# Moving an indexer's choice of keys ahead of the latent up-projections, and filling latent heads to 128 rows

## The chip, the cores and the metric

The kernel runs on one core of a Trainium2 chip. The metric is the device time of one execution in microseconds (us). An engine's instructions run in the order of its queue; the order is laid out when the kernel is built. The engines are TensorE (PE; its weight loads are listed as PEld), VectorE (DVE), ScalarE (ACT), GpSimd (POOL) and SyncE (SP, which issues the loads of weights).

## The reference, cut to what matters

Two blocks of two layers each run one after the other on 256 positions of width 1024, all in float32. The first block has feed-forward parts, window attention and retention, and the change does not touch it. A layer of the second block projects its input, runs three kinds of attention side by side, gates the result, projects it out and normalizes. The change concerns two of the three:

- Latent attention has 6 heads. The queries come from a normalized vector of 768 values through an up-projection, the keys and values from one of 256. A head's query and key are 64 plain values and 32 rotated ones, 96 in all.
- Sparse attention has 4 heads. An indexer picks for each query the 64 best keys, and only those take part:

```python
logits = einsum('bqhd,bsd->bqhs', qib, k_idx) * IDX_DIM ** -0.5
score = einsum('bqh,bqhs->bqs', wb * IDX_HEADS ** -0.5, relu(logits))
score = where(key_pos <= qpos, score, -inf)
_, idx = top_k(score, topk)
```

The third kind, dilated attention with 6 heads, follows behind both.

## The kernel before, in words

A stage is one part of one layer; stages follow each other, and the two last stages, one for each layer of the second block, are those of class `Mixer2`. Positions lie in two tiles of 128 (tile 0 and tile 1). Products with weights are exact to float32 through three products of high and low parts: `get_at` (lines 298 to 308) loads a piece of weights, ScalarE writes its high part (line 304) and VectorE its low part (line 306). Eight buffers of each part let two groups of weights be in work. Results of TensorE go to eight banks: two with the name `mm` for projections, two `tr` for transposes, four `ac` for scores and attention outputs. Each bank has to be emptied by ScalarE or VectorE before its next use.

Nobody writes the order of a queue out by hand. The program issues instructions in the order of its text, and the builder lays out each engine's queue by its own estimate of when each instruction can start. `issue_after` ties some instructions behind others where the author wanted that.

`Mixer2.body` (line 1165) runs, in the order of its text:

- the indexer's query projection (`post2`), transposes of the latent vectors, then `post3` (indexer and sparse keys) and `post4` (line 1192: rotated latent key, the indexer's head weights, sparse values);
- the latent query up-projection, lines 1202 to 1214: two halves by two tiles, each in one `mm` bank, emptied by one ScalarE copy and by the four VectorE steps of `rope` (lines 647 to 650);
- the latent key and value up-projection, lines 1215 to 1226, also four `mm` banks;
- the transposes of queries and keys, lines 1236 to 1240, 96 columns to a head, into the tiles qT and kT, of which 96 partitions are used;
- latent scores (`a_score`, from `make`, line 1088): a matmul for each head with 96 rows, then `softmax` (line 652), whose first VectorE step, line 655, empties the bank;
- between them `choose(0)` (line 1278) and `choose(1)` (line 1283), and behind each the next projections as they fit.

`choose` (line 1041) makes the selection of one tile. TensorE multiplies 8 indexer heads in pairs on 64 rows each (line 1053); ScalarE takes the relu into one of two buffers `rl` (line 1057); VectorE adds the heads up with their weights in a chain of eight steps (lines 1063 and 1065), adds the causal mask, and then finds 64 keys in eight rounds: the top 8 (line 1069) and their replacement by a low value (line 1070). Two more steps make a mask. The sparse scores `c_score(0)` and `c_score(1)` (lines 1293 and 1298) use these masks.

Of the kernel before, what the change touches and what calls it, by code (L numbers as in the profile page):

```python
# [9 lines left out]
F32 = mybir.dt.float32  # L10
# [929 lines left out]
class Mixer2(OutProj, Attn):  # L940
# [100 lines left out]
    def choose(self, t, qiT):  # L1041

        K, nc = self.K, self.K.nc
        nk = 128 + 128 * t
        nh = 512 // nk
        acc = self.scr.tile([128, 256], F32, tag=f"acc{t}", name="acc")[:, :nk]
        cau = K.cau[:, 0:128] if t == 0 else K.cau[:, 128:384]
        for p0 in range(0, 4, nh):
            ps = [K.bank("ac", 4) for _ in range(2)]
            for j in range(nh):  # L1050
                for e in range(2):
                    r = slice(64 * e, 64 * e + 64)
                    K.mm(ps[e][:, nk * j:nk * j + nk], lhsT=qiT[r, p0 + j, 128 * t:128 * t + 128], rhs=self.kiT[r, :nk],
                         start=True, stop=True)
            for e in range(2):
                rl = self.rl[:, e]
                nc.scalar.activation(out=rl, in_=ps[e], func=AF.Relu, scale=0.125)
                for j in range(nh):
                    h = 2 * (p0 + j) + e
                    r = rl[:, nk * j:nk * j + nk]  # L1060
                    w = self.wi[:, t, h:h + 1]
                    if h == 0:
                        nc.vector.tensor_scalar(out=acc, in0=r, scalar1=w, scalar2=None, op0=ALU.mult)
                    else:
                        nc.vector.scalar_tensor_tensor(out=acc, in0=r, scalar=w, in1=acc, op0=ALU.mult, op1=ALU.add)  # L1065
        nc.vector.tensor_tensor(out=acc, in0=acc, in1=cau, op=ALU.add)
        m8 = K.small([8], "m8", 4)
        for _ in range(8):
            nc.vector.max(out=m8, in_=acc)  # L1069
            nc.vector.match_replace(out=acc, in_to_replace=m8, in_values=acc, imm_value=-3.0e38)  # L1070
        nc.vector.tensor_scalar(out=acc, in0=acc, scalar1=-2.0e38, scalar2=NEG, op0=ALU.is_gt, op1=ALU.mult)
        nc.vector.tensor_tensor(out=acc, in0=acc, in1=cau, op=ALU.add)
        self.sel[t] = acc
# [91 lines left out]
    def body(self):  # L1165
        K, nc, d = self.K, self.K.nc, self.K.d
        scr = self.scr
# [30 lines left out]
            self.copy(0, self.vc[:, t, :], ps[:, 40:296])  # L1198

        self.proj(post4)  # L1200

        for j in range(2):
            p = K.get(2)
            for t in range(2):
                ps = K.bank("mm")
# [10 lines left out]
        for t in range(2):  # L1216
            for j in range(2):
                ps = K.bank("mm")
# [6 lines left out]
                else:  # L1225
                    self.copy(1, self.va[:, t, :], ps[:, :384])

        self.rl = self.keep.tile([128, 2, 512], F32, tag="ch0", name="rl")
        self.al = self.keep.tile([128, 2, 512], F32, tag="cl0", name="al")
        self.n_al = 0  # L1230
        qbT = self.keep.tile([128, 4, 256], F32, tag="ch1", name="qbT")
# [1 line left out]
        vb = vbt.rearrange("p a n -> p (a n)")[:, :768].rearrange("p (t n) -> p t n", t=2)  # L1233
        qT = self.keep.tile([128, 6, 256], F32, tag="qT", name="qaT")
        kT = scr.tile([128, 6, 256], F32, tag="kT", name="kaT")
        for t in range(2):
            for dst, src, e in ((qT, qa[t], 0), (kT, ka[t], 1)):
                for h0, n in ((0, 4), (4, 2)):
                    ps = K.transposes([src[:, 96 * h:96 * h + 96] for h in range(h0, h0 + n)])
                    self.copy(e, dst[:96, h0:h0 + n, ts(t)], ps[:96, :128 * n].rearrange("p (h n) -> p h n", h=n))  # L1240
        self.y = [scr.tile([128, 4, 256], F32, tag=f"cqx{a}", name=f"y{a}") for a in range(2)]
        a_score, a_av = self.make(6, (64 + 32) ** -0.5, lambda h, s, q=qT: q[:96, h, s],
                                  lambda h, nk, k=kT: k[:96, h, :nk], self.va, 0, self.caus, False)
        half = lambda x: lambda h, s: x[64 * (h % 2):64 * (h % 2) + 64, h // 2, s]
        keys = lambda x: lambda h, nk: x[64 * (h % 2):64 * (h % 2) + 64, h // 2, :nk]
        c_score, c_av = self.make(4, 0.125, half(self.qcT), keys(self.kcT), self.vc, 3,
# [28 lines left out]

        a_score(0)
        a_score(1)
        self.choose(0, self.qiT)
        self.proj_T(4, post5)
        self.together(a_av(0), a_av(1))  # L1280
        a_score(2)
        a_score(3)
        self.choose(1, self.qiT)
        a_score(4)
        kbT = scr.tile([128, 3, 256], F32, tag="kT", name="kbT")

# [22 lines left out]
        for q in range(2):  # L1309
            ps = K.bank("tr")  # L1310
            for i in range(4):
                k = 16 + 4 * q + i
# [80 lines left out]
```

## Time and profile before

| | us |
|---|---|
| median of 3 runs | 1330.25 |
| lowest and highest | 1329.29, 1332.18 |
| the profiled execution, own time | 1329.58 |
| its span, first to last instruction | 1327.8 |
| busy: TensorE, VectorE, ScalarE, GpSimd | 1308.1, 1022.9, 741.2, 25.2 |
| mean granted TensorE clock | 0.998 |

Times in the trace count from the span's start. Matmuls are pipelined: a matmul's duration is longer than the step to the next one's start, so steps between starts are what a group costs. A float32 product without the split shows as two records. The stage of the first layer lies at about 966 to 1138 us, that of the second one about 178 us later. A row of the timeline merges neighbours of one kind: its first number is the start, the second the time to the end of the last one.

### The profile page before, as it was taken

How to read it: one execution, taken by the hardware profiler on the slowest of the kernel's cores; microseconds unless marked ns; L12 is line 12 of the kernel's file. 1: busy time of each engine (PE TensorE's matmuls, PEld its weight loads, DVE VectorE, ACT ScalarE, POOL GpSimd, SP SyncE). 2: the span in 40 equal slices, each digit the busy share in tenths (PEclk: the TensorE clock that was granted, in tenths of full speed). 3: DMA queues.
4: the chain of work that ended last, by engine and by line, in shares of the span. 5: the costliest groups of instructions: out<-in, count | busy, mean ns of one | idle time of the engine just before them, and what ended most of it. 6: DMA issues, size and time to landing. Idle time of an engine off the chain costs nothing. (4 is left out here: it accounts for less than half of the span.)

```text
span 1327.8 us, 20378 instructions
## 1 busy us (share of the span) xinstructions
PE 1308.1 (99%) x7606; PEld 1128.1 (85%) x7606; DVE 1022.9 (77%) x1753; ACT 741.2 (56%) x1312; POOL 25.2 (2%) x34
## 2 busy tenths in 40 slices
PE   9999999999999999999999999999999999999997
PEld 8888887888888888888887878888889898799886
DVE  7777669978976769787589777677585797866976
ACT  7755536446544546555355555545455678356681
POOL 0000000000000000000000000000000000000000
PEclk9999999999999999999999999999999999999999
DMA  9987624637867728877433548678355434364420
GB/s 330 342 302 266 211 75 143 211 123 259 310 234 260 252 81 327 278 263 249 151 128 114 204 139 286 206 269 275 127 176 181 139 127 145 126 209 160 142 81 33
DMA packets 75923, 263.39 MB, mean 198 GB/s; under 512 B 9104, under 2 KB 10384, under 8 KB 75696
## 3 DMA queue, kind: packets, MB, share of 16 engines
q1 hardware_dynamic: 74736, 259.75, 57.2%
q0 software_dynamic: 512, 1.69, 0.4%
q8 instruction: 59, 0.97, 0.3%
q10 hardware_dynamic: 576, 0.66, 0.1%
q14 instruction: 40, 0.33, 0.1%
HBM read 261.01 MB, written 1.05 MB: 197 GB/s over the span
## 5 line engine op out<-in xcount | busy, mean ns | idle before, releaser
L306 DVE TENSOR_TENSOR wlo<-st,whi 128x1024 fp32r<-128x1024 f32 (+5 forms) x320 | 372.3, 1174 | 66.6 <-ACT whi L304 66.3
L304 ACT ACTIVATE whi<-st 128x1024 fp32r<-128x1024 f32 (+5 forms) x320 | 322.8, 1018 | 115.3 <-DMA st<-in_w 45.7
L327 PE MATMUL mm<-xx,whi 128*128 128x256 f32 (+1 forms) x1296 | 333.7, 333 | 0.0
L327 PE MATMUL mm<-xx,wlo 128*128 128x256 f32 x928 | 261.7, 283 | 0.0
L327 PEld LDWEIGHTS mm<-xx,whi 128*128 128x128 f32 x1296 | 220.2, 190 | 24.2 <-issue 0.3
L327 PE MATMUL mm<-whi,xx 128*128 128x512 f32 (+3 forms) x744 | 219.4, 372 | 0.6 <-DVE xx L374 0.4
L327 PE MATMUL tr<-xx,whi 128*128 128x512 f32 x560 | 195.8, 392 | 0.0
L327 PEld LDWEIGHTS mm<-xx,wlo 128*128 128x128 f32 x928 | 176.6, 190 | 2.0 <-DVE wlo L306 0.4
L327 PE MATMUL tr<-xx,wlo 128*128 128x256 f32 x560 | 156.6, 280 | 0.0
L327 PEld LDWEIGHTS mm<-whi,xx 128*128 128x128 f32 x744 | 135.0, 188 | 24.8 <-DVE xx L374 1.7
L306 DVE TENSOR_TENSOR xlo<-st,xhi 128x1024 fp32r<-128x1024 f32 x106 | 128.4, 1218 | 18.8 <-ACT xhi L304 18.1
L304 ACT ACTIVATE xhi<-st 128x1024 fp32r<-128x1024 f32 x106 | 109.9, 1054 | 50.5 <-PE ac L327 39.2
L327 PE MATMUL mm<-wlo,xx 128*128 128x512 f32 (+3 forms) x372 | 137.1, 369 | 0.0
L327 PE MATMUL ac<-xlo,hth 128*128 128x512 f32 x320 | 125.6, 393 | 0.0
L327 PE MATMUL ac<-xhi,hth 128*128 128x512 f32 x320 | 125.4, 392 | 0.0
L327 PEld LDWEIGHTS tr<-xx,whi 128*128 128x128 f32 x560 | 104.8, 187 | 23.1
L327 PEld LDWEIGHTS tr<-xx,wlo 128*128 128x128 f32 x560 | 105.9, 189 | 1.3
L327 PE MATMUL ac<-xhi,htl 128*128 128x512 f32 x320 | 104.4, 391 | 0.0
L316 DVE SCALAR_TENSOR_TENSOR st<-st,sc 128x1024 f32<-128x1024 f32 x48 | 58.6, 1222 | 53.2 <-DMA st<-in_w 53.1
L327 PEld LDWEIGHTS mm<-wlo,xx 128*128 128x128 f32 x372 | 70.1, 188 | 10.6 <-issue 0.3
L373 ACT ACTIVATE hth<-sa 128x256 fp32r<-128x256 f32 x76 | 31.4, 413 | 79.1 <-DVE sa L538 79.0
L327 PEld LDWEIGHTS ac<-xhi,hth 128*128 128x128 f32 x320 | 60.1, 188 | 14.3
(271 smaller groups left out, 1829.0 us busy)
## 6 DMA issues: line engine op xcount, KB each, us to landing
st<-in_w SPq DMA_DIRECT2D x441, 512.0 KB, 4.6
st<-in_w SPq DMA_DIRECT2D x20, 384.0 KB, 3.6
g<-in_lng SPq DMA_DIRECT2D x8, 512.0 KB, 4.5
b<-in_lnb SPq DMA_DIRECT2D x8, 512.0 KB, 5.6
st<-in_w SPq DMA_DIRECT2D x8, 432.0 KB, 4.0
st<-in_w SPq DMA_DIRECT2D x8, 296.0 KB, 4.7
st<-in_w SPq DMA_DIRECT2D x5, 256.0 KB, 5.5
x<-in_x SPq DMA_DIRECT2D x2, 512.0 KB, 7.7
```

The source lines that it names most:

```text
L304: nc.scalar.activation(out=hi[:, :m], in_=st[:, :m], func=AF.Copy)
L306: nc.vector.tensor_tensor(out=lo[:, :m], in0=st[:, :m], in1=hi[:, :m].bitcast(F32), op=ALU.subtract)
L316: nc.vector.scalar_tensor_tensor(out=st, in0=st, scalar=1.0, in1=self.sc, op0=ALU.mult, op1=ALU.mult, accum_out=self.mod[l][:, j:j + 1])
L327: return self.nc.tensor.matmul(*a, **k).ins
L373: nc.scalar.activation(out=hi, in_=src, func=AF.Copy)
```

## The change

`choose` for both tiles moves from among the latent scores to just behind `post4`, ahead of the latent up-projections. Tile 0 takes its two banks from `tr`, tile 1 its four from `ac`. The relu buffers become three, and they lie in the memory that kT takes afterwards. Apart from that, qT and kT have their last 32 partitions cleared on GpSimd; the transposes take 128 columns (the last head 96), and the latent scores 128 rows.

```diff
         nk = 128 + 128 * t
         nh = 512 // nk
+        tag = (("tr", 2), ("ac", 4))[t]
         acc = self.scr.tile([128, 256], F32, tag=f"acc{t}", name="acc")[:, :nk]
...
-            ps = [K.bank("ac", 4) for _ in range(2)]
+            ps = [K.bank(*tag) for _ in range(2)]
...
-                rl = self.rl[:, e]
+                rl = self.rl[:, self.n_rl % 3]
+                self.n_rl += 1
...
         self.proj(post4)
+        self.rl = scr.tile([128, 3, 512], F32, tag="kT", name="rl")
+        self.n_rl = 0
+        self.choose(0, self.qiT)
+        self.choose(1, self.qiT)
...
-        self.rl = self.keep.tile([128, 2, 512], F32, tag="ch0", name="rl")
...
         kT = scr.tile([128, 6, 256], F32, tag="kT", name="kaT")
+        for a in (qT, kT):
+            nc.gpsimd.memset(a[96:128], 0.0)
...
-                    ps = K.transposes([src[:, 96 * h:96 * h + 96] for h in range(h0, h0 + n)])
+                    ps = K.transposes([src[:, 96 * h:min(96 * h + 128, 576)] for h in range(h0, h0 + n)])
...
-        a_score, a_av = self.make(6, (64 + 32) ** -0.5, lambda h, s, q=qT: q[:96, h, s],
-                                  lambda h, nk, k=kT: k[:96, h, :nk], self.va, 0, self.caus, False)
+        a_score, a_av = self.make(6, (64 + 32) ** -0.5, lambda h, s, q=qT: q[:, h, s],
+                                  lambda h, nk, k=kT: k[:, h, :nk], self.va, 0, self.caus, False)
...
         a_score(0)
         a_score(1)
-        self.choose(0, self.qiT)
         self.proj_T(4, post5)
         self.together(a_av(0), a_av(1))
         a_score(2)
         a_score(3)
-        self.choose(1, self.qiT)
         a_score(4)
```

## Rows read from the trace of the kernel before

**Rows 1.** The page, busy time of each engine over the span (share, instructions).

```profile
PE 1308.1 (99%) x7606; PEld 1128.1 (85%) x7606; DVE 1022.9 (77%) x1753; ACT 741.2 (56%) x1312; POOL 25.2 (2%) x34
```

**Rows 2.** Busy time by stretch: PE, PEld, DVE, ACT, POOL (instructions), granted clock, DMA share, GB/s.

```profile
1020.00:1030.00 10.00, 10.00 (x77) 10.00 (x77) 8.96 (x24) 6.13 (x10) 0.00 (x0) 1.00 0.67 218
1030.00:1040.00 10.00, 9.95 (x71) 9.28 (x70) 6.45 (x14) 5.98 (x11) 0.00 (x0) 1.00 0.55 172
...
1060.00:1070.00 10.00, 10.00 (x80) 9.85 (x80) 9.86 (x34) 9.04 (x21) 0.00 (x0) 1.00 0.01 2
```

**Rows 3.** TensorE's waits, 966 to 1138: us in total, times, longest.

```profile
PE ac L327 <- ACT PT L687: 0.9, 2, 0.5
```

**Rows 4.** Timeline of TensorE around tile 0's indexer scores.

```profile
1040.04 1.06 PE L327 MATMUL ac<-kaT,qaT 96*128 96x128 f32 x8
1041.03 1.16 PE L327 MATMUL ac<-kk,qiT 64*128 64x128 f32 x16
1042.12 0.38 PE L327 MATMUL mm<-xx,wlo 128*128 128x256 f32 x1
```

**Rows 5.** Timeline of TensorE around tile 1's indexer scores (idle time before, and its releaser).

```profile
1056.90 1.56 PE L327 MATMUL ac<-kk,qiT 64*128 64x256 f32 x10
1058.98 1.13 PE L327 MATMUL ac<-kk,qiT 64*128 64x256 f32 x6 [0.53 <-DVE P L655]
1060.04 1.13 PE L327 MATMUL ac<-kaT,qaT 96*128 96x256 f32 x4
```

**Rows 6.** Weight loads by line, 1030 to 1055: busy us, mean ns, idle before.

```profile
L442 PEld LDWEIGHTS tr<-idn,ka 128*96 128x96 f32 x12 | 1.2, 126 | 0.4 <-ACT qaT L1037 0.4
...
L442 PEld LDWEIGHTS tr<-idn,P 128*128 128x128 f32 x6 | 0.7, 140 | 0.0
```

**Rows 7.** Timeline of VectorE with both choices under way.

```profile
1060.21 0.08 DVE L1070 MATCH_VALUE_LOAD acc<-m,acc 128x8 f32 x1
1060.29 0.27 DVE L1070 MATCH_REPLACE8 acc<-m,acc 128x128 f32<-128x128 f32 x1
1060.48 0.47 DVE L1065 SCALAR_TENSOR_TENSOR acc<-rl,kk,acc 128x256 f32<-128x256 f32 x1
1060.87 0.28 DVE L1069 MAX8 m<-acc 128x8 f32<-128x128 f32 x1
1061.08 0.48 DVE L1065 SCALAR_TENSOR_TENSOR acc<-rl,kk,acc 128x256 f32<-128x256 f32 x1
```

**Rows 8.** Timeline of VectorE, tile 0's choice beside latent scores.

```profile
1058.06 0.28 DVE L1069 MAX8 m<-acc 128x8 f32<-128x128 f32 x1
1058.26 0.67 DVE L655 SCALAR_TENSOR_TENSOR P<-ac,cau 128x512 f32<-128x512 f32 x1
```

**Rows 9.** VectorE's groups by line and shape, 1042 to 1083: busy us, mean ns.

```profile
L1069 DVE MAX8 m<-acc 128x8 f32<-128x256 f32 x8 | 3.4, 420 | 0.1
...
L1070 DVE MATCH_REPLACE8 acc<-m,acc 128x256 f32<-128x256 f32 x8 | 3.3, 409 | 0.0
```

**Rows 10.** Timeline: first query tile, its first rotary step, first record behind the fourth.

```profile
1021.33 0.29 PE L327 MATMUL mm<-whi,ch 128*128 128x288 f32 x1
...
1024.50 0.25 DVE L647 TENSOR_TENSOR qa<-mm,rt 128x96 f32<-128x96 f32 x1
...
1030.86 0.33 PE L327 MATMUL mm<-whi,ch 128*128 128x384 f32 x1
```

**Rows 11.** Timeline of TensorE in the first microseconds; one stretch at the end (columns of rows 2).

```profile
6.19 0.63 PE L327 MATMUL mm<-xx,whi 128*128 128x512 f32 x1
...
6.83 0.53 PE L327 MATMUL mm<-xx,whi 128*128 128x512 f32 x1
...
9.97 0.40 PE L327 MATMUL mm<-xx,whi 128*128 128x512 f32 x1
...
10.32 0.40 PE L327 MATMUL mm<-xx,whi 128*128 128x512 f32 x1
...
1322.00:1324.00 2.00, 0.00 (x0) 0.00 (x0) 2.00 (x4) 0.00 (x0) 0.32 (x1) 0.50 0.00 0
```

## The prediction

> **What bounds the kernel now.** I read the page first: TensorE is busy 99% of the span [rows 1]. A change must take matmul time or waits out of its queue, and whatever makes it wait is paid in full. Next comes busy time by stretch for the first of the two stages that the change touches (the second repeats it 178 us later). There the reader is to see VectorE: 9.0 of 10 us busy at 1020 to 1030, 6.5 at 1030 to 1040, full at 1060 to 1070, where both choices now run [rows 2]. Then TensorE's waits and timeline: in this stage it loses little to others, 0.9 us to transposed weights of the softmax (PT) and a wait of 0.53 us inside tile 1's scores [rows 3, 5].
>
> **Zero rows and columns.** Matmuls with 96 rows come every 0.11 us (8 in 1.06 us, the last of them 0.275) and the switch to them costs nothing visible; the pass to 64 rows does cost: the next group starts 0.21 us after the last 96-row start [rows 4]. A 128-column operand streams no longer with 128 rows than with 96, so the scores gain 0. For the transposes the weights grow from 96 to 128 columns; a load then takes 140 ns in place of 126, beside other matmuls [rows 6]: 0. By the Trainium skill (TensorEngine Tiling (Array Packing), Key Properties) a change of tiling mode drains TensorE. If 96 rows were a mode of its own, the zero rows would save such a drain at each latent group; [rows 4] shows one only at 64 rows. By the Trainium skill (TensorE: Matmul & The Clock Gate, LDWEIGHTS) a load takes its columns over 1.2 GHz, an estimate of 27 ns more for each of 20 transposes a stage, 1.1 us over both, if nothing hid it; [rows 6] shows 14 ns, and hidden.
>
> The two clears of 32 partitions by 1536 values on GpSimd have no like in the trace; from below they cost nothing, as GpSimd is idle in this stretch [rows 2], from above about 1 us a stage if a score waits. I take 0, since 10 us lie between the last use of the relu buffers and the first latent score. The second clear does stand behind those buffers, in the same memory; so do the copies of the latent keys.
>
> **Scores of the indexer moved.** The 16 matmul records of tile 0 stand from 1041.03 to 1042.12, 1.09 us for eight pairs of 0.105; with 0.10 at entry that is 0.35 us of overhead [rows 4]. Tile 1's visit lasts from 1056.90 to 1060.04, 3.14 us for eight pairs of 0.21 (1.7), with its wait for a bank that VectorE had not emptied; entry adds 0.1, so 1.5 us of overhead [rows 5]. Afterwards the visits join, all six banks are free, and one overhead of 0.35 stays: 1.5 us a stage saved. I add 0.5, the longest of the PT waits, for a VectorE that is then freer [rows 3]; bounds 0 and 0.9.
>
> **The choice moved: VectorE's queue.** This term decides. Each choice is one chain: eight multiply-adds, then eight rounds of top-8 and replace. How long do both take when they run through each other? Beside tile 1's multiply-adds a round of tile 0 takes 0.08 + 0.19 + 0.21 = 0.48 us from start to start, and a multiply-add of 256 values 0.39 [rows 7]. Start to start is some 0.08 less than the durations; so a round of tile 1 is 0.34 + 0.07 + 0.33 = 0.74 [rows 9], and a multiply-add of 128 about 0.2 (a 128-wide step less the overlap; alone in its chain 0.35). Tile 0: 8 x 0.2 + 8 x 0.48 + 0.5 = 6.0. Tile 1: 8 x 0.39 + 8 x 0.74 + 0.9 = 9.9. Together 15.9 us.
>
> Who stands behind them? VectorE runs its queue in the order laid out at build time. What that order does with two live chains stands in [rows 7]: replace of tile 0, multiply-add of tile 1, top-8 of tile 0, multiply-add of tile 1, nothing between. An evacuation that the program issues after tile 0's choice goes one step of the chain later, while TensorE waits 0.53 us for it [rows 5, 8]. So I read: what the program issues first goes first, and later work enters only where no chain has a step ready. The diff now issues both choices before the latent queries' up-projection, whose four rotary steps on VectorE [rows 10] empty its bank. There are two such banks for four tiles.
>
> The four query tiles now follow each other from 1021.33 to 1030.86, 2.38 us each [rows 10]. Afterwards the scores take 0.85 + 1.75 + 0.35 = 3.0 us first; tiles 1 and 2 end near 1026.7 and 1029.1. The first choice starts near 1023.5 (its scores end at 1022.4, a relu of 0.6 follows). Neither choice issues a load. Until about 1031 tile 1's chain waits for relu buffers, so tile 0 leaves gaps: some casts of weights (1.2 us each) and the rotary steps of query tile 1 get through near 1030. From then both chains fill VectorE until tile 0's ends: 1023.5 + 15.9 + 3.5 for what slipped in, less 3 that tile 1 has left, near 1040. The rotary steps of query tile 2 wait so long. TensorE runs tile 3 from 1030.2 to 1032.6 and then has no bank: about 0.9 + 7.6 = 8.5 us idle a stage. If tiles 2 and 3 slip through it is 2; if nothing does, 12 (1029.1 to 1041). Both are bounds. ScalarE's relus and SyncE's loads are not late then: casts for the next group stand behind the chains as well, but are needed only after the idle time, and four of them need 5 us.
>
> A long idle time costs clock. At the end of the run, where TensorE has no work left, the granted clock is 0.50 (1.2 GHz) from 1322 on [rows 11]. In the first microseconds a pair of matmuls comes every 0.64 us, later every 0.35 [rows 11]: until 7.2 TensorE, at work since 1.1, loses some 3 us. I take 2 us a stage, between 0 (idle time broken up) and 3.
>
> **Sum.** 8.5 + 2 - 1.5 - 0.5 = 8.5 us a stage, 17 over both. The profiled execution took 1329.6 us; 1346.6, and 1347 against the median, which is 0.7 above it. Own range: 2 x (2 + 0 - 2) = 0 to 2 x (12 + 3 - 1.5) = 27, so 1330 to 1357.
>
> **Rivals.** *The evacuations get through.* Then only the savings stay: 2 x 1.5 to 2 x 2, 1326 to 1327. For it: a rotary step is 0.1 to 0.2 us and only four are wanted per tile; at 1062 to 1066 later work did enter between steps of one chain. Against: there one chain was done or waited. It decides where both chains end before 1033, when the third tile's evacuation is due, or where the queue favours what TensorE waits for. Chance 0.19. A drain at each change to 96 rows, the rule above, belongs here: some eight changes a stage at 0.1 to 0.35 us would give 2 to 5 us more, 1322 to 1325; [rows 4] speaks against it, 0.02 of the 0.19.
>
> *Both effects cancel.* Idle time of about 2 us a stage in short pieces, without loss of clock, against 1.5 to 2 saved: 1330. For it: VectorE has 4.6 us free in 20 us [rows 2]. Against: 15.9 do not fit there. Chance 0.10.
>
> *The change to the choice does little,* because the tile 0 scores are held back by the two transposition banks and run late: TensorE then works on as before. These banks were emptied ten microseconds earlier, so I give it only 0.01 within the last.
>
> **Numbers.** A measurement of this kernel tells about 0.2% (2.7 us) from no change. Forecast 0.71, cancelling 0.10, evacuations through 0.19. Nearly all of the forecast's range lies above 1333, so slower 0.70, same 0.11, faster 0.19. To leave out no more than 2 in 10 the range takes in the cancelling case and half of the faster one: 1326 to 1357.
>
> **What will show it.** Right: in the new trace TensorE idles for several microseconds among the query up-projections of each stage, ended by VectorE's rotary steps, with top-8 and replace steps of both tiles before them; the granted clock falls there; scores of both tiles stand in one group; spacing of the latent scores is unchanged at 0.11. Wrong: rotary steps between choice steps near 1027 to 1033 and TensorE full; or the idle time ended by a late weight cast.

## The result, and the profile of the changed kernel

The changed kernel takes 1350.1 us (median of 4 runs, 1349.0 to 1351.3), against 1330.1 for the kernel before (median of 4). The ratio is 1.0151, 95% interval 1.0139 to 1.0163: slower by 1.5%, against a forecast of 1347 us within 1326 to 1357. The profiled execution took 1350.49 us with a span of 1348.5, 20.7 us above the span before.

The page of the changed kernel, busy time of each engine, answers to [rows 1]:

```profile
PE 1308.5 (97%) x7606; PEld 1131.2 (84%) x7606; DVE 1024.4 (76%) x1753; ACT 743.4 (55%) x1312; POOL 30.8 (2%) x38
```

TensorE's instructions are as many as before, and its busy time moved by only 0.4 us, since what a slower clock adds to it is saved elsewhere. Its share fell from 99% to 97%, and 20.3 of the 20.7 us are idle time. Where it lies shows in busy time by stretch (the columns are those of [rows 2]), for the first stage:

```profile
1020.00:1030.00 10.00, 9.64 (x82) 8.77 (x80) 9.45 (x25) 7.04 (x13) 0.00 (x0) 1.00 0.57 185
1030.00:1040.00 10.00, 0.00 (x0) 0.00 (x0) 10.00 (x50) 1.84 (x3) 1.37 (x1) 0.63 0.00 0
1040.00:1050.00 10.00, 8.76 (x47) 8.68 (x48) 7.72 (x29) 2.63 (x5) 0.00 (x0) 0.69 0.26 81
1041.00:1046.00 5.00, 4.76 (x20) 4.79 (x21) 4.21 (x13) 0.06 (x1) 0.00 (x0) 0.50 0.18 50
...
1060.00:1070.00 10.00, 10.00 (x86) 10.00 (x85) 4.38 (x10) 8.23 (x25) 0.00 (x0) 1.00 0.16 51
```

For ten full microseconds TensorE issues nothing while VectorE is busy for all of them. Part of that work came from 1060 to 1070, where VectorE was full before [rows 2] and is now busy for 4.38 of 10 us. TensorE's waits of the stage, 966 to 1150 (us in total, times, longest), name what it waited for:

```profile
PE mm L327 <- DVE tmp L649: 11.6, 1, 11.6
PE tr L442 <- ACT P L1111: 0.4, 2, 0.2
PE ac L327 <- DVE P L655: 0.4, 1, 0.4
PE mm L327 <- DVE xx L374: 0.2, 1, 0.2
```

One wait holds everything: a bank `mm`, released by line 649, the third rotary step and the last of the four that reads the bank. The second stage has the same wait, also 11.6 us. The same view of the kernel before, whose largest row is [rows 3], goes on with these:

```profile
PE ac L327 <- DVE P L655: 0.9, 2, 0.5
PE ac L327 <- ACT y L1037: 0.4, 1, 0.4
```

So the waits other than the new one went from 2.6 us (0.9 + 0.9 + 0.4 and two of 0.2) to 1.0. TensorE's timeline of the changed kernel around the wait (start, time, then operation; idle time and its releaser in brackets):

```profile
1021.79 1.16 PE L327 MATMUL tr<-kk,qiT 64*128 64x128 f32 x16
1022.78 1.90 PE L327 MATMUL ac<-kk,qiT 64*128 64x256 f32 x16
1024.61 0.40 PE L327 MATMUL mm<-whi,ch 128*128 128x288 f32 x1
...
1029.35 0.29 PE L327 MATMUL mm<-whi,cl 128*128 128x288 f32 x1
1041.24 0.58 PE L327 MATMUL mm<-whi,ch 128*128 128x288 f32 x1 [11.60 <-DVE tmp L649]
1041.62 0.44 PE L327 MATMUL mm<-wlo,ch 128*128 128x288 f32 x1
1041.86 0.44 PE L327 MATMUL mm<-whi,cl 128*128 128x288 f32 x1
...
1046.18 0.35 PE L327 MATMUL mm<-whi,cl 128*128 128x288 f32 x1
1046.37 0.29 PE L327 MATMUL mm<-whi,ch 128*128 128x288 f32 x1
1046.50 0.29 PE L327 MATMUL mm<-wlo,ch 128*128 128x288 f32 x1
```

The reader sees three things. The scores of both tiles stand together, 2.82 us from 1021.79 to 1024.61. Then two query tiles, two banks, and the stop. And behind the stop matmuls come every 0.24 us until 1046.18, then every 0.13: for 5 us the granted clock is 0.50, or 1.2 GHz, to which it had fallen in the idle time. VectorE's timeline in the stop and at its end:

```profile
1037.11 0.30 DVE L1072 MATCH_REPLACE8 acc<-m,acc 128x128 f32<-128x128 f32 x1
1037.30 0.64 DVE L1071 MAX8 m<-acc 128x8 f32<-128x256 f32 x2
...
1039.36 0.28 DVE L1074 TENSOR_TENSOR acc<-acc,cau 128x128 f32<-128x128 f32 x1
1039.56 0.42 DVE L1071 MAX8 m<-acc 128x8 f32<-128x256 f32 x1
1039.89 0.24 DVE L647 TENSOR_TENSOR qa<-mm,rt 128x96 f32<-128x96 f32 x1
1040.05 0.08 DVE L1072 MATCH_VALUE_LOAD acc<-m,acc 128x8 f32 x1
1040.12 0.41 DVE L1072 MATCH_REPLACE8 acc<-m,acc 128x256 f32<-128x256 f32 x1
1040.44 0.20 DVE L648 TENSOR_TENSOR tmp<-mm,rt 128x48 f32<-128x48 f32 x1
1040.56 0.43 DVE L1071 MAX8 m<-acc 128x8 f32<-128x256 f32 x1
1040.91 0.19 DVE L649 TENSOR_TENSOR tmp<-mm,rt 128x48 f32<-128x48 f32 x1
```

Until then steps of both tiles follow each other with nothing between. The first rotary step comes 0.25 us after tile 0's choice has ended with line 1074, and from then on one rotary step stands behind each step of the chain that is left. It is the first query tile's: its bank had been full since about 1027.

It could not have come at 1027, though. A tile's first rotary step waits for ScalarE's copy of the same tile, and the relus of tile 1 stood ahead of that copy in ScalarE's queue, waiting for buffers that the multiply-adds (line 1067) had not read yet. Three rows of ScalarE's timeline, and one of VectorE's that shows the dependence at the third tile:

```profile
1026.83 1.09 ACT L1059 ACTIVATE rl<-ac 128x512 f32<-128x512 f32 x2 [1.97 <-DVE acc L1067]
1028.91 0.60 ACT L1059 ACTIVATE rl<-ac 128x512 f32<-128x512 f32 x1 [0.99 <-DVE acc L1067]
1029.40 0.32 ACT L1037 ACTIVATE qa<-mm 128x192 f32<-128x192 f32 x1
...
1046.30 0.26 DVE L647 TENSOR_TENSOR qa<-mm,rt 128x96 f32<-128x96 f32 x1 [1.09 <-ACT qa L1037]
```

So the first tile's rotary steps were held by ScalarE until 1029.72, and by VectorE's order from there to 1039.89.

**The sum.** By stage: the new wait 11.6; 20 matmuls at half clock from 1041.24 to 1046.18, 4.94 us where 20 x 0.133 = 2.66 would do, so 2.28 lost; the scores 2.82 in place of 1.09 + 3.14 [rows 4, 5], 1.4 saved; the other waits 1.6 saved, of which 0.5 lay inside the scores. That is 11.6 + 2.28 - 1.4 - 1.1 = 11.4, 22.8 over both stages. The spans differ by 20.7, of which 0.36 lies ahead of the first stage (the same record of `post4` starts at 1014.77 before and at 1015.13 now). So some 2 us of savings, about 1 a stage, are not accounted for.

### The profile page after: what moved, and what is told of

Its sections match the earlier page's. It is cut to its first block, busy times and chain, and to the rows that moved or that the text cites. A ratio compares the mean times of both kernels' runs of the same rounds, so it can differ in the third digit from the quotient of the medians.

```text
span 1348.5 us, 20374 instructions
## 1 busy us (share of the span) xinstructions
PE 1308.5 (97%) x7606; PEld 1131.2 (84%) x7606; DVE 1024.4 (76%) x1753; ACT 743.4 (55%) x1312; POOL 30.8 (2%) x38
## 4 chain that ended last, share of the span: by engine, by line
PE 84%; DVE 10%; ACT 2%; issue 2%; DMA 1%; POOL 1%; SPq 0%; DVEq 0%; POOLq 0%; ACTq 0%
PE mm L327 39%; PE ac L327 27%; PE tr L327 14%; PE tr L442 3%; DVE wlo L306 2%; DMA st<-in_w 1%; DVE acc L1067 1%; DVE acc L1072 1%; POOL rs_y L385 1%; DVE P L655 1%; DVE m L1071 1%; ACT whi L304 1%; DVE xlo L306 1%; DVE x L407 1%; ACT P L666 1%
## 5 line engine op out<-in xcount | busy, mean ns | idle before, releaser
L306 DVE TENSOR_TENSOR xlo<-st,xhi 128x1024 fp32r<-128x1024 f32 x106 | 128.6, 1220 | 20.3 <-ACT xhi L304 20.2
L327 PEld LDWEIGHTS ac<-xhi,htl 128*128 128x128 f32 x320 | 60.1, 188 | 12.8
```

Of the source, the lines that this page charges most:

```text
L306: nc.vector.tensor_tensor(out=lo[:, :m], in0=st[:, :m], in1=hi[:, :m].bitcast(F32), op=ALU.subtract)
L327: return self.nc.tensor.matmul(*a, **k).ins
```

## Experiments

Each kernel is told by its edit and set beside the kernel before on the same chip. The code shown is cut, and from experiment 3 on it is a difference from the changed kernel.

**1. The zero rows alone.** The kernel before, with the clears, the 128 columns and the 128 rows; the choice stays.

> Zero rows and 128 columns alone, the choice left among the latent scores. Theory (they cost and save nothing that matters): 1329 to 1331 us, ratio 0.999 to 1.001, latent scores still 0.11 us apart, transposes still about 0.11. Rival (a drain at each change to 96 rows goes, the lower rival of the prediction): 2 to 5 us less, 1325 to 1328. Rival (longer weight loads show): 1 us or more above 1331.

1329.84 us against 1329.92, ratio 0.9999 (0.9990 to 1.0008). TensorE's timeline in this kernel, to be set beside [rows 4]:

```profile
1040.51 0.87 PE L442 MATMUL tr<-idn,ka 128*128 128x128 f32 x6
1041.22 1.06 PE L327 MATMUL ac<-kaT,qaT 128*128 128x128 f32 x8
1042.21 1.16 PE L327 MATMUL ac<-kk,qiT 64*128 64x128 f32 x16
```

Eight records with 128 rows take 1.06 us, and the next group starts 0.99 after their start, as with 96 rows. The six transposes ahead take 0.71 to the first score. In the kernel before, with 96 columns and a change to 96 rows, they took 0.70, from this row to the first of [rows 4]:

```profile
1039.34 0.86 PE L442 MATMUL tr<-idn,ka 128*96 128x128 f32 x6
```

The weight loads went to 140 ns:

```profile
L442 PEld LDWEIGHTS tr<-idn,qa 128*128 128x128 f32 x10 | 1.2, 140 | 0.1
```

So this half of the change is worth nothing either way.

**2. The choice alone.** The changed kernel with the latent heads left at 96.

> Choice moved as in the change, latent heads left at 96 rows and columns. Theory (the whole loss is the choice's): idle of about 11.6 us a stage among the query up-projections, half clock for some 5 us behind it, 1348 to 1352 us. Rival (clears, wider loads or 128 rows have a share of the loss): 1 us or more below the whole change, under 1348 us.

1350.12 us, ratio 1.0153 (1.0139 to 1.0166), with the same wait of 11.6 us in each stage. The whole loss is the choice's.

**3 and 4. One of the two choices early.** The other goes back to its old place, with its two old relu buffers.

```diff
         self.choose(0, self.qiT)
-        self.choose(1, self.qiT)
...
         a_score(3)
+        self.choose(1, self.qiT)
         a_score(4)
```

> Whole change, but only tile 0's choice early; tile 1's stays behind the fourth latent score. Theory (two live chains fill VectorE and starve the rotary steps; one chain alone leaves a place behind each of its steps): TensorE idles under 1 us among the query up-projections of a stage, 1327 to 1331 us. Rival (any choice that the program issues first holds the rotary steps until it ends, one chain as well): tile 0's chain ends some 8 to 10 us after its start, the idle time is 4 to 6 us a stage and with lost clock the kernel takes 1340 to 1346 us.

> Whole change, but only tile 1's choice early; tile 0's stays behind the second latent score. Theory (one chain alone leaves places): idle under 2 us a stage among the query up-projections, 1327 to 1333 us. Rival (one chain starves as well): its 11 to 13 us hold the banks for 6 to 8 us a stage, 1345 to 1350 us.

Tile 0 early: 1329.16 us, ratio 0.9994 (0.9985 to 1.0003). Tile 1 early: 1329.18, ratio 0.9993 (0.9984 to 1.0002). Neither can be told from the kernel before. VectorE's timeline with tile 0's chain alone:

```profile
1026.17 0.25 DVE L647 TENSOR_TENSOR qa<-mm,rt 128x96 f32<-128x96 f32 x1
1026.34 0.34 DVE L1067 SCALAR_TENSOR_TENSOR acc<-rl,kk,acc 128x128 f32<-128x128 f32 x1
1026.60 0.20 DVE L648 TENSOR_TENSOR tmp<-mm,rt 128x48 f32<-128x48 f32 x1
1026.72 0.35 DVE L1067 SCALAR_TENSOR_TENSOR acc<-rl,kk,acc 128x128 f32<-128x128 f32 x1
1026.99 0.20 DVE L649 TENSOR_TENSOR tmp<-mm,rt 128x48 f32<-128x48 f32 x1
```

A rotary step stands between steps of the chain, and TensorE loses 0.2 us to them in this stretch. With tile 1's, the longer chain, it is 1.2 + 0.6. One chain leaves a place behind each step; in the changed kernel the second chain takes that place. ScalarE's copy of the first query tile comes early too, at 1025.51 and 1025.72, so these two kernels change ScalarE's queue as well; the next one leaves that copy late, at 1029.24.

**5. One chain behind the other.** Both stay ahead in the text with their priority. Only the first multiply-add of tile 1 is queued behind tile 0's last step.

```diff
                     if h == 0:
-                        nc.vector.tensor_scalar(out=acc, in0=r, scalar1=w, scalar2=None, op0=ALU.mult)
+                        with K.tc.issue_after(self.end0) if t else nullcontext():
+                            nc.vector.tensor_scalar(out=acc, in0=r, scalar1=w, scalar2=None, op0=ALU.mult)
```

> Whole change, text order and priorities as they are, but tile 1's chain on VectorE begins only behind the last step of tile 0's. Theory (two chains that are live together leave no place; one leaves a place behind each step): the rotary steps of the first query tile come near 1030 and those of the second near 1033, so TensorE idles about 1.2 + 0.8 = 2 us a stage in two pieces, no half clock, 1327 to 1333 us. Rival (whatever the program issues first is run first, so 16 us of choice ahead in the text cost the same in any order): idle 10 us or more a stage, 1345 to 1352 us.

1329.17 us, ratio 0.9995 (0.9986 to 1.0004). One wait of 2.1 us a stage, ended by line 649; VectorE's timeline in it:

```profile
1030.43 0.29 DVE L1072 MAX8 m<-acc 128x8 f32<-128x128 f32 x1
...
1031.14 0.29 DVE L1072 MAX8 m<-acc 128x8 f32<-128x128 f32 x1
1031.36 0.24 DVE L647 TENSOR_TENSOR qa<-mm,rt 128x96 f32<-128x96 f32 x1
...
1031.77 0.20 DVE L648 TENSOR_TENSOR tmp<-mm,rt 128x48 f32<-128x48 f32 x1
1031.89 0.29 DVE L1072 MAX8 m<-acc 128x8 f32<-128x128 f32 x1
```

A round alone takes 0.71 us from top-8 to top-8 (1030.43 to 1031.14), and with two rotary steps in it 0.75 (1031.14 to 1031.89): the places are there. The rotary steps could have used them from 1029.57 on, when ScalarE's copy of their tile had ended (here too it stood behind a relu that waited for a buffer), but come at 1031.36, two rounds and a top-8 later. The order of the queue is laid down when the kernel is built; why the builder put them there is not shown. So the 16 us of choice cost next to nothing when only one chain is live, although both still come first in the text. The forecast of "no half clock" was a miss; it is told with the surprises below.

**6. Both choices further down.** They stand behind the query up-projection, ahead of that of keys and values.

> Whole change, but both choices stand in the text behind the latent query up-projection, ahead of the key and value up-projection. Theory (the two chains hold whatever evacuation on VectorE comes next in the text): the query tiles run through, and the idle time goes to the key and value up-projection, ended by the copy of latent values: scores end near 1034, three tiles and some transposes later, near 1038, TensorE stops until the copy gets through near 1047, 8 to 10 us a stage with half clock behind it, 1343 to 1351 us. Rival (it was the query tiles' own four rotary steps, a longer evacuation, that did it): under 3 us a stage, 1325 to 1333 us.

1344.85 us, ratio 1.0115 (1.0102 to 1.0129). TensorE's waits of the first stage:

```profile
PE mm L327 <- DVE va L1039: 6.4, 1, 6.4
PE mm L327 <- ACT ka L1037: 1.9, 1, 1.9
```

The wait follows the choice, 8.3 us in two pieces. The larger piece is for the next evacuation on VectorE, the copy of the latent values. The smaller one is for ScalarE's copy of the keys, at 1037.50, behind relus that waited for the multiply-adds in part. The larger piece ends at 1048.75; it stands ahead of the next projection and not among the value tiles, since transposes and the last tiles still got in. The rotary steps as such are not the cause.

**7. The bank emptied by ScalarE.** The rotary columns go to a small buffer first.

```diff
+                raw = tt[:, 96:192]
+                self.copy(0, raw.rearrange("p (h w) -> p h w", h=3), pv[:, :, 64:96])
...
-                self.rope(sp(o), sp(pv), ...)
+                self.rope(sp(o), raw.rearrange("p (h e w) -> p h e w", h=3, e=2), ...)
```

> Whole change, but ScalarE copies the rotary columns of a query tile out of its bank (into one of two small buffers), and the rotary steps on VectorE read that copy. Theory (TensorE waits for a bank, and the bank for VectorE): all four query tiles run through to near 1034; then the third tile's copy waits for a buffer that the first tile's rotary steps hold, these come near 1041 as in the change, and TensorE idles 6 to 8 us a stage in place of 11.6, at another place, ahead of the key and value up-projection; 1338 to 1344 us. Rival (TensorE waits for VectorE's results, the transposes of the queries, or for weights' low parts, not for banks): idle still 11 us or more in the same place, 1348 us or more.

1342.05 us, ratio 1.0092 (1.0077 to 1.0107). TensorE's timeline and the wait:

```profile
1034.95 0.29 PE L327 MATMUL mm<-whi,cl 128*128 128x288 f32 x1
1042.03 0.47 PE L442 MATMUL tr<-idn,qa 128*128 128x128 f32 x1 [6.79 <-DVE qa L650]
```

All four query tiles run through, so it was the bank that stopped them. The size of the next stop is as expected, 6.8 us, but what it waits for is the rotary result itself: a transpose of the first query tile is the next in TensorE's queue. Of the rival, the transposes are true for the second wait and not for the first.

**8. The choice with a later priority.** Scores and relus stay early; the builder ranks the VectorE steps of both choices as if they stood 300 instructions further down.

```diff
-                for j in range(nh):
+                with K.tc.high_priority(offset=-300):
+                  for j in range(nh):
...
-        nc.vector.tensor_tensor(out=acc, in0=acc, in1=cau, op=ALU.add)
...
+        with K.tc.high_priority(offset=-300):
+            nc.vector.tensor_tensor(out=acc, in0=acc, in1=cau, op=ALU.add)
...
```

> Whole change, but the multiply-adds, top-8 and replace steps of both choices carry a priority as if they stood 300 instructions later in the text; scores and relus stay early. Theory (only the place of the rotary steps in VectorE's queue costs time): TensorE's idle time of 11.6 us a stage goes, granted clock stays at 1.00, and the savings of joined scores remain: 1322 to 1329 us. Rival (VectorE has not the time for 16 us of choice in this stretch, whatever the order): the idle time moves to the key and value up-projections or the transposes, over 4 us a stage, 1338 us or more. Rival (the scores' six banks, held until the relus are through, stop TensorE): waits for tr or ac banks of several us, 1335 us or more.

1328.0 us, ratio 0.9985 (0.9976 to 0.9994), the granted clock at 1.00 throughout the stage. VectorE is busy for 10.0 of 10 us at 1030 to 1040 here too, and TensorE loses 1.9 us to the rotary steps in place of 11.6. Both chains are live here as well, so it is not their number alone but their place ahead of the rotary steps in VectorE's queue that cost the time. This also bounds what ScalarE's late copy costs: it ends at 1029.51, the first query tile's rotary steps begin at 1029.99, and the wait that they end is 1.2 us.

**9 to 11. Looking for a version that beats both.** In the first, the rounds stand in the text behind the rotary steps of the first and the last query tile and are queued behind them. The second also moves tile 1's scores and multiply-adds behind the first query tile's rotary steps; tile 0's rounds then stand behind the second query tile's, and tile 1's behind tile 0's. The third moves the second four of these multiply-adds behind the second tile's rotary steps.

```diff
+                if j == t:
+                    with K.tc.issue_after(r.ins):
+                        self.pick(t)
```

> Whole change, but the rounds of top-8 and replace stand in the text behind the rotary steps of the first query tile (tile 0's) and of the last one (tile 1's) and are queued behind these on VectorE; scores, relus and multiply-adds stay early. Theory: one chain at a time beside the evacuations, idle under 1 us a stage among the query up-projections, no half clock, the savings of the joined scores remain: 1323 to 1328 us. Rival (VectorE is then late for the latent scores instead): waits for ac banks or PT of more than 2 us a stage, 1329 us or more.

> As picks_tied, but tile 1's scores and multiply-adds stand behind the first query tile's rotary steps, and its rounds behind those of tile 0. Theory: the rotary steps of the first query tile then come before 1028, so the idle time of 1.7 us a stage that picks_tied still has goes to under 0.5, against 0.3 us for a visit of the indexer's scores that is no longer joined: 1324 to 1327 us. Rival (the second query tile's rotary steps are now late, behind 3 us of multiply-adds and a cast of 1.2): idle of 2 us a stage stays, 1327 to 1330 us.

> As picks_apart, but the second four of tile 1's multiply-adds stand behind the second query tile's rotary steps. Theory (in picks_apart these steps came 1.7 us late because seven multiply-adds of some 0.5 us and a cast of 1.2 stood ahead of them): four multiply-adds fewer ahead, so the steps come near 1031.5 in place of 1033.2, the idle time of 1.7 us a stage goes, and the kernel takes 3.4 us less than picks_apart, 1323 to 1326 us. Rival (the wait moves on, to the later rotary steps or to the second half's banks): 1326 to 1329 us.

1327.31 us (0.9980, 0.9971 to 0.9989); 1327.47 (0.9980, 0.9971 to 0.9989); 1326.65 (0.9979, 0.9970 to 0.9989). All three beat both kernels by a little, and cannot be told apart. The first is in its range, though it loses 1.9 us a stage where under 1 was expected; the other two lie just above theirs, in those of their rivals. Each removal of a wait brought another: in the first kernel 1.7 us at the third query tile; in the second 1.7 us at the fourth, where the rival was right, the second tile's steps waiting behind seven multiply-adds and a cast; in the third these steps came at 1031.47, as expected, and the wait, now 1.3 us, went on to the first tile of keys and values, as its rival had it.

So some 0.2% is what the move is worth when the queue is right.

## Why the prediction was right, point by point

- **Zero rows and columns, 0.** Right: experiment 1. The rule of the Trainium skill (TensorEngine Tiling (Array Packing), Key Properties), a drain at a change of mode, doesn't show at a change from 128 to 96 rows: 0.70 us for six transposes ahead of such a change, 0.71 without one. The load's rule of the Trainium skill (TensorE: Matmul & The Clock Gate, LDWEIGHTS) put an estimate of 1.1 us on the wider loads if nothing hid them. So small a loss lies within the interval of experiment 1; the trace speaks against it, with loads longer by 14 ns and transposes that follow each other as before. The clears took 1.37 us on GpSimd, at 1032.13 in the changed kernel, and nobody waits for them.
- **Scores joined, 1.5 a stage.** Right: 1.4. **A freer VectorE, 0.5, up to 0.9:** the PT waits of 0.9 us are gone altogether; with the small ones 1.1.
- **The choice's two chains hold the rotary steps.** Right in engine, line, place and reason; experiments 3 to 6 and 8 vary these. ScalarE's part is left out. The two chains' own steps were sized fairly: 17.5 us from 1024.87 to 1042.37, with five rotary steps in it, against 15.9 for the chains alone. That tile 0's end came at 1039.6 against "near 1040" is in part luck: the chains began 1.4 us later than forecast, behind two casts, and took longer, and of the 3.5 us that were to slip in between them nothing did.
- **8.5 us of idle time.** Too small: 11.6. The step that failed is that the rotary steps of query tile 1 "get through near 1030", in gaps that tile 0's chain leaves while tile 1 waits for relu buffers. They did not get in; they came at 1039.89, and so TensorE stopped after two tiles and not three. That is the upper bound of the prediction, 12, where "nothing does". Two things stood against it. ScalarE's relus "are not late then", the prediction says, but they waited 1.97 and 0.99 us for buffers, and the copy behind them ended only at 1029.72, the earliest time for these rotary steps. By then the gaps were closed: tile 1 had its last relu at 1029.51, not "about 1031", and its multiply-adds went on at 1029.54. Whether the steps would have got in between two live chains with an earlier copy, no run shows. (The 8.5 stands as 0.9 + 7.6; by the prediction's own times it is 1.1 + 7.4, the same sum.)
- **2 us of clock.** Right: 2.3, between the bounds of 0 and 3.
- **The sum, 17.** It came nearer to the 20.7 than its idle time does, because the savings were 0.5 us a stage larger than forecast and about 1 more a stage stands in no term.
- **The rivals.** "The evacuations get through" is what happens with one chain (1329.2) or with a later priority (1328.0), not here. Its first point of decision, both chains ended before 1033, was not the one that counted. Its second, a queue that favours what TensorE waits for, is what experiment 8 brings about; one live chain at a time is another way. Its price, 1326 to 1327, is close to the 1326.7 to 1327.5 of the last three kernels. "Both effects cancel" is close to experiment 5, where 2.1 us of idle time and, in some executions, up to 1.5 us of clock stand against the savings.

## What to carry to other kernels

On an engine that runs its queue in order, a chain of dependent short steps leaves places for other work, and two such chains that come first in its order leave none. Before such work is moved ahead, ask which evacuations stand behind it in the text and how many banks cover them; two banks of 2.4 us each do not cover 16. Ask it of every engine that empties the bank: here ScalarE's copies stood behind relus that waited for the same chains. The early part of the work (here the scores) can be moved without the late part, by a priority or an explicit order, and a full engine then does little harm (experiment 8).

## What had not been expected of the hardware

The granted clock can fall after the idle time, when TensorE is at work again. In experiment 5 TensorE waits 2.1 us, resumes at 1032.44 with a matmul every 0.13 us, and then slows down to 0.50, or 1.2 GHz (busy time by stretch; the last three columns are granted clock, DMA share and GB/s):

```profile
1032.00:1033.00 1.00, 0.56 (x4) 0.59 (x5) 0.96 (x7) 0.00 (x0) 0.00 (x0) 1.00 0.00 0
1033.00:1034.00 1.00, 1.00 (x8) 1.00 (x7) 1.00 (x3) 0.00 (x0) 0.00 (x0) 0.76 0.00 0
1034.00:1035.00 1.00, 1.00 (x6) 1.00 (x5) 1.00 (x6) 0.00 (x0) 0.00 (x0) 0.50 0.00 0
```

From 1033.44 to 1036.94 fourteen matmuls and a transpose take 3.5 us where 14 x 0.133 + 0.1 = 2.0 would do, so 1.5 us came on top of a wait of 2.1. It seems not to come in every execution: the mean granted clock of the whole span lies between 0.995 and 0.998 in the ten runs of this kernel. The two at 0.998 took 1327.7 and 1328.6 us, the four at 0.995 or 0.996 took 1329.4 to 1330.4. In the first kernel of experiments 9 to 11 a wait of 1.73 us at the same place, ended at 1032.41, left the clock as it was (0.998 or 0.999 over the span in all eleven runs):

```profile
1030.00:1035.00 5.00, 3.27 (x26) 3.06 (x24) 4.66 (x23) 2.88 (x5) 1.38 (x1) 1.00 0.00 0
1035.00:1040.00 5.00, 4.75 (x33) 4.27 (x32) 5.00 (x22) 3.28 (x6) 0.00 (x0) 1.00 0.27 82
```

The wait of 11.6 us cost 2.3 us of clock, against 1.5 for that of 2.1.
